# Query norms moved behind the scores, norm weights folded into the rotary tables, and one gate unit fewer in each head of an encoder kernel

## The chip, the cores and the metric

The kernel runs on one core of one Trainium2 chip. The metric is the time of one execution on the device, in microseconds; before the change its median is 1917.95 us over 3 runs (1914.27 to 1920.34).

## What is computed

One encoder layer, applied to two requests of 1024 tokens and width 1024 that share the weights ("prompt", g = 0, and "sample", g = 1). The input is normalised and modulated, and one projection `w_in` gives everything else. Branch A is attention with 8 query and 2 key heads of 64; branch B has 4 heads with two 64-wide softmax maps each and 128-wide values. Both normalise queries and keys head by head (RMSNorm with a weight) and turn them by rotary positions. Each branch is multiplied by a SiLU gate and projected, the two are merged with sigmoid gates, and a last projection with a gated residual gives the output. What the change touches:

```python
qa = rms_norm(qa.reshape(B, S, HQ_A, HEAD_DIM), qn_a)   # per head: x * rsqrt(mean(x*x) + EPS) * weight
ka = rms_norm(ka.reshape(B, S, HKV_A, HEAD_DIM), kn_a)
qa = concat(apply_rope(qa[..., :32], cos_r, sin_r), apply_rope(qa[..., 32:], cos_c, sin_c))   # ka too
oa = gqa_attention(qa, ka, va) * silu(za)               # softmax(q k / 8) v
qb = rms_norm(qb.reshape(B, S, H_B, 2, HEAD_DIM), qn_b)
kb = rms_norm(kb.reshape(B, S, H_B, 2, HEAD_DIM), kn_b)
qb = concat(apply_rope(qb[..., :16], cos_p, sin_p), qb[..., 16:])                             # kb too
ob = diff_attention(qb, kb, vb, lam)                    # (softmax(q1 k1 / 8) - lam * softmax(q2 k2 / 8)) v
```

## The kernel before

The work of a request runs in this order. **Head** (`head`): `kva_gen` projects A's keys and values, `qa_gen(st, 0)` the first four query heads of A. **Attention** (`attention`): 16 units of branch A in two halves, then 16 units of branch B, four for each head; while one half or head is attended, the projections of the next (`qa_gen(st, 1)`, `vb_gen`, `qkb_gen`) are woven in. **Then** the gating (`gated_gen`), the merge (`merge_gen`) and the output projection, `out_gen` for g = 0 and `out_seven` for g = 1. The gate projections, `z_gen`, are 48 units a request of 24 matmuls each; nothing waits for them until the gating, so they are the stock from which TensorE is kept busy wherever another chain is late. `Z_HEAD` (L41) says how many of them the head takes, `Z_SHARE` how many each phase of the attention, and what is left goes into the last phase (`fill`).

A projection (`pipelined`, L601) goes by 8 token tiles. `proj_tt` issues 24 matmuls of 128x256 for a tile (L540); `front` does the norm and the rotation on ScalarE, VectorE and GpSimd; `back`, two tiles later (`LAG` = 2), transposes the tile on TensorE and splits it into two parts (`pairs_T`, L594 to L597). In `front`, `rms` (L551) copies the tile out of PSUM (L555), squares it (L556), sums the squares by head (L559), adds EPS (L560), takes the power -0.5 on GpSimd (L561) and multiplies every head by its inverse rms (L563). Then come the norm's weight (L643 for A's keys, L662 for A's queries, L681 for B's queries and keys) and `rope`: L574 times the cosines, L582 twice times the sines, L583 the sum. L563 and what follows run on VectorE while nothing is attended (`alone`, so in the heads) and on GpSimd during attention.

A softmax unit (`softmax_unit`, L741) is one query tile of one map: four matmuls of 128x512 (L747, L748) fill one of the two `s` banks of PSUM, VectorE takes the negated row maximum (L749), ScalarE the exponential with that maximum as its bias and the row sum as a second output (L750), VectorE transposes the result (L791, after a combination at L790 in branch B), and DMAs (L800) bring it into the order that the value matmuls (L806, L823) read. There are 256 of these units.

The kernel is written as generators that `weave` interleaves by shares. A scheduler then sets the order of the instructions on each engine, and attention's steps are given a high priority there. Every engine works through its own list in order, and the DMAs are issued in order by SyncE's queue (SP). The other work of GpSimd is the split of each weight piece into two parts (L195, L237). L775 is a reciprocal of a row sum, L325 the projections of the modulation, L359, L416 and L417 its use on the activations.

Of the kernel before, what the change touches and what calls it, by code (L numbers as in the profile page):

```python
# [12 lines left out]
F32 = mybir.dt.float32  # L13
# [27 lines left out]
Z_HEAD = (4, 4)  # L41
# [48 lines left out]
def kernel(ctx: ExitStack, tc: tile.TileContext, t: dict):  # L90
# [330 lines left out]
    cosB = const.tile([P, NTT, 16], F32, name="cosB")  # L421
    sinB = const.tile([P, NTT, 16], F32, name="sinB")
# [13 lines left out]

    def load_tables_B():
# [113 lines left out]
    def rms(ps, nh, e):  # L551
# [6 lines left out]
        rs = tiny.tile([P, 4], F32, tag="rs", name=nm("rs"))[:, :nh]  # L558
# [4 lines left out]
        e.tensor_tensor(  # L563
            out=raw3, in0=raw3, in1=rs.unsqueeze(2).to_broadcast([P, nh, HD]), op=ALU.mult
        )
        return raw3, sq.rearrange("p (h d) -> p h d", d=HD)

    def rope(x3, s3, cos, sin, half, e):

        nh = x3.shape[1]  # L570
        w = x3.shape[2]
        ng = w // (2 * half)
        c3 = mtile("rc", [P, 4, HD], bufs=1)[:, :nh, :w]
        e.tensor_tensor(out=c3, in0=x3, in1=cos.unsqueeze(1).to_broadcast([P, nh, w]), op=ALU.mult)  # L574
        if ng == 1:
            x4, s4, sn = x3, s3, sin.unsqueeze(1).to_broadcast([P, nh, w])
        else:
            x4, s4 = (t.rearrange("p h (g d) -> p h g d", g=ng) for t in (x3, s3))
            sn = sin.rearrange("p (g d) -> p g d", g=ng).unsqueeze(1).to_broadcast([P, nh, ng, 2 * half])
        for a in range(2):  # L580
            o, i = (slice(b * half, (b + 1) * half) for b in (a, 1 - a))
            e.tensor_tensor(out=s4[..., o], in0=x4[..., i], in1=sn[..., o], op=ALU.mult)  # L582
        e.tensor_tensor(out=x3, in0=c3, in1=s3, op=ALU.add)  # L583
# [48 lines left out]
    def kva_gen(ht, out):  # L632
        w = kva_w.pop()[0] if kva_w else load_w(w_cols(w_in, (C_KA, 256)))
        k = v2(utile())
        va = utile().bitcast(F32)[:, :1024].rearrange("p (n k d) -> p n k d", n=NTT, k=2)
        out["ka"], out["va"] = k, va

# [15 lines left out]
    def qa_gen(st, half):  # L653
        w = load_w(w_cols(w_in, (C_QA + half * 256, 256)))
        qs = [v2(utile()), v2(utile())]
        ht = st["ht"]
        st["qa"][half] = qs

        def front(tt, ps):
            e = by_turns(tt)  # L660
            x3, s3 = rms(ps, 4, e)
            e.tensor_tensor(out=x3, in0=x3, in1=gqa.unsqueeze(1).to_broadcast([P, 4, HD]), op=ALU.mult)  # L662
            rope(x3, s3, st["cosA"][:, tt], st["sinA"][:, tt], 16, e)
            return x3
# [8 lines left out]
    def qkb_gen(ht, out, h):  # L673
        w = load_w(w_cols(w_in, (C_QB + h * P, P), (C_KB + h * P, P)))
        qk = out[h] = (v2(utile()), v2(utile()))

        def front(tt, ps):
            e = by_turns(tt)
            x3, s3 = rms(ps, 4, e)
            x4 = x3.rearrange("p (a m) d -> p a m d", a=2)  # L680
            e.tensor_tensor(out=x4, in0=x4, in1=gB.unsqueeze(2).to_broadcast([P, 2, 2, HD]), op=ALU.mult)  # L681
            rope(x3[:, :, :16], s3[:, :, :16], cosB[:, tt], sinB[:, tt], 8, e)
# [58 lines left out]
    def softmax_unit(q, sw, k, pt, su):  # L741
# [3 lines left out]
        for n in range(2):  # L745
# [3 lines left out]
        nc.vector.tensor_reduce(out=m, in_=s, axis=AX.X, op=ALU.max, negate=True)  # L749
        nc.scalar.activation(  # L750
            pt.rearrange("p (j c a) -> p j c a", j=4, c=8), s.rearrange("p (c a j) -> p j c a", c=8, j=4),
            AF.Exp, bias=m, accum_out=su,
        )

    def scores(u, i):
# [11 lines left out]
        softmax_unit(u["q"][m][:, qt * P : (qt + 1) * P], u["sw"][:, m, t * P : (t + 1) * P], u["k"][m], pt, su)  # L767
# [402 lines left out]
    def units_of(st):  # L1170

        def a_unit(half, b, pr):
# [5 lines left out]
                "pr": pr, "od": st["od"][j // 2], "su": st["suA"][:, j : j + 2],  # L1178
            }

        def b_unit(h, pr):
# [3 lines left out]
                "v": st["vb"][h], "pr": pr, "h": h,  # L1185
                "od": st["od"][4 + h], "ss": st["ssB"], "su": st["suB"][:, h],
# [38 lines left out]
    for g in range(2):  # L1225
# [21 lines left out]
        phase(1, vb_gen(ht, st["vb"], 0), qkb_gen(ht, st["qkb"], 0))  # L1247
        oT, mT = ([], []), ([], [])
        for h in range(4):
            fs = []  # L1250
            if h < 3:
                fs.append(qkb_gen(ht, st["qkb"], h + 1))
# [84 lines left out]
```

## Time and profile before

| what | value |
|---|---|
| time of 3 runs, us | 1914.27, 1917.95, 1920.34 (median 1917.95) |
| time of the profiled execution, us | 1911.4 |
| its span in the trace, us | 1909.6 |
| TensorE matmuls busy | 1847.3 us, 97% of the span |
| TensorE weight loads busy | 1553.5 us, 81% |
| VectorE (DVE) busy | 1209.3 us, 63% |
| ScalarE (ACT) busy | 771.6 us, 40% |
| GpSimd (POOL) busy | 666.6 us, 35% |
| granted TensorE clock, mean share of full speed | 0.986 |
| where things lie, us from the span's start | head of g = 0 from about 48 to 140, A's attention to about 457, B's to 765; head of g = 1 from 982 to about 1063, A's to 1360, B's to 1719 |

The profile is of one execution. A group's row gives, behind the count, the busy time in us, the mean of one instruction in ns, and the idle time of the engine just before such instructions with what ended it. In the table of waits a row says which engine and line waited for which, with the total in us, the number of waits and the longest. A tile's name stands without its number: `s` are the banks of the scores, `f` the other PSUM banks, `row` the tile under normalisation, `p` the exponentials, `m` the row maxima, `w` split weights, `u` large buffers.

### The profile page before, as it was taken

What the parts mean: (1) busy time and instruction counts of PE and PEld (TensorE: products, weight loads), DVE (VectorE), ACT (ScalarE), POOL (GpSimd) and SP (SyncE); (2) the same over time, 40 slices, a digit from 0 to 9 for tenths busy, and PEclk for the clock granted to TensorE, in tenths of its full rate; (3) what the DMA queues carried; (4) which work ended last, traced back from release to release, by engine and by line L of the source; (5) the groups of instructions that cost most, each with busy time, mean ns of one, the idle gap of its engine ahead of it and who ended that gap; (6) DMA issues with size and microseconds to landing.
All of it is one profiled execution on the core that took longest, in us unless ns stands there. A gap on an engine that the chain in (4) does not pass through costs nothing.

```text
span 1909.6 us, 29522 instructions
## 1 busy us (share of the span) xinstructions
PE 1847.3 (97%) x10398; PEld 1553.5 (81%) x10398; DVE 1209.3 (63%) x1791; ACT 771.6 (40%) x1576; POOL 666.6 (35%) x904
## 2 busy tenths in 40 slices
PE   6999999999999999999999999999999899999999
PEld 3788778888888978788888877888898798877887
DVE  5777753454876667457467787445366746674795
ACT  4545443443554444213233455344354535332241
POOL 2234511442654551221232343024474736212100
PEclk7999999999999999999999999999999999999999
DMA  9126675554443557864531567665434424586442
GB/s 320 57 84 163 186 199 159 161 151 141 111 123 104 161 152 229 281 183 156 200 107 51 146 188 196 183 182 161 138 92 115 129 70 109 163 254 211 147 126 90
DMA packets 273044, 295.04 MB, mean 155 GB/s; under 512 B 35200, under 2 KB 221696, under 8 KB 272896
## 3 DMA queue, kind: packets, MB, share of 16 engines
q1 hardware_dynamic: 272896, 293.15, 51.8%
q8 instruction: 83, 1.36, 0.3%
q14 instruction: 65, 0.53, 0.1%
HBM read 133.59 MB, written 42.01 MB: 92 GB/s over the span
## 4 chain that ended last, share of the span: by engine, by line
PE 74%; DMA 7%; DVE 6%; SPq 4%; issue 4%; POOL 3%; ACT 2%; DVEq 0%; ACTq 0%; POOLq 0%
PE f L713 20%; PE f L540 17%; PE f L985 5%; PE a L806 5%; PE s L747 5%; PE s L748 5%; PE a L823 4%; PE s L985 3%; PE f L1020 3%; SPq L800 2%; PE s L1020 2%; DMA st<-in_w_in_dram 2%; PE f L1092 2%; DVE m L749 2%; PE s L1092 1%
## 5 line engine op out<-in xcount | busy, mean ns | idle before, releaser
L713 PE MATMUL f<-u,w 128*128 128x512 f32 x2256 | 582.2, 398 | 2.7 <-POOL w L195 1.2
L713 PEld LDWEIGHTS f<-u,w 128*128 128x128 f32 x2256 | 416.5, 189 | 88.9 <-POOL w L195 2.4
L540 PE MATMUL f<-w,u 128*128 128x256 f32 x3456 | 477.8, 287 | 1.3 <-ACT w L193 0.3
L540 PEld LDWEIGHTS f<-w,u 128*128 128x128 f32 x3456 | 452.4, 192 | 22.1 <-issue 3.5
L749 DVE TENSOR_REDUCE m<-s 128x1 f32<-128x1024 f32 x256 | 310.3, 1219 | 200.0 <-PE s L748 198.0
L750 ACT ACTIVATE p<-s,m 128x1024 f32<-128x1024 f32 x256 | 285.1, 1114 | 279.0 <-DVE m L749 238.8
L195 POOL TENSOR_TENSOR w<-st,w 128x512 fp32r<-128x512 f32 x160 | 215.8, 1366 | 441.1 <-ACT w L193 424.8
L791 DVE STREAM_TRANSPOSE p<-p 128x1024 f32<-128x1024 f32 x192 | 237.6, 1241 | 58.0 <-ACT p L750 50.0
L561 POOL TENSOR_TENSOR rs<-ss,nhalf 128x4 f32<-128x4 f32 (+1 forms) x112 | 110.0, 983 | 308.7 <-DVE ss L560 271.8
L748 PE MATMUL s<-u,sw 128*128 128x512 f32 x512 | 203.8, 399 | 0.0
L193 ACT ACTIVATE w<-st 128x512 fp32r<-128x512 f32 x184 | 108.2, 627 | 98.1 <-DMA st<-in_w_in_dram 83.3
L985 PE MATMUL f<-u,w 128*128 128x512 f32 x552 | 134.8, 398 | 2.3 <-DVE u L1000 2.3
L823 PE MATMUL a<-q,u 128*128 128x256 f32 x512 | 127.0, 385 | 8.9 <-DMA q<-p 4.2
L985 PEld LDWEIGHTS f<-u,w 128*128 128x128 f32 x552 | 105.0, 192 | 24.6 <-DVE u L1000 2.5
L597 DVE TENSOR_TENSOR u<-f,u 64x256 fp32r<-64x256 f32 (+1 forms) x194 | 79.7, 411 | 71.3 <-ACT u L596 66.4
L806 PE MATMUL a<-q,u 128*64 128x256 f32 x1024 | 117.8, 382 | 2.0 <-DMA q<-p 2.0
L823 PEld LDWEIGHTS a<-q,u 128*128 128x128 f32 x512 | 95.3, 192 | 24.5 <-issue 7.6
L747 PE MATMUL s<-u 128*128 128x512 f32 x256 | 106.5, 418 | 4.9 <-ACT p L750 4.9
L748 PEld LDWEIGHTS s<-u,sw 128*128 128x128 f32 x512 | 97.2, 190 | 16.8
L790 DVE SCALAR_TENSOR_TENSOR p<-p,r,p 128x1024 f32<-128x1024 f32 x64 | 91.3, 1427 | 28.5 <-POOL r L776 26.8
L806 PEld LDWEIGHTS a<-q,u 128*64 128x64 f32 x1024 | 73.4, 137 | 40.3 <-issue 6.9
L747 PE MATMUL s<-u,u 128*128 128x512 f32 x256 | 102.9, 402 | 1.4 <-ACT p L750 1.4
(215 smaller groups left out, 2032.3 us busy)
## 6 DMA issues: line engine op xcount, KB each, us to landing
q<-p SPq DMA_DIRECT2D x768, 128.0 KB, 2.6
st<-in_w_in_dram SPq DMA_DIRECT2D x132, 256.0 KB, 3.2
zd<-ev SPq DMA_DIRECT2D x96, 256.0 KB, 2.7
sw<-u SPq DMA_DIRECT2D x256, 64.0 KB, 2.0
u<-in_w_ada_dram SPq DMA_DIRECT2D x8, 1024.0 KB, 11.4
od<-oo SPq DMA_DIRECT2D x64, 128.0 KB, 2.4
st<-in_w_in_dram SPq DMA_DIRECT2D x64, 128.0 KB, 2.7
row<-od SPq DMA_DIRECT2D x32, 256.0 KB, 2.9
```

What stands on the lines that cost most here:

```text
L195: e.tensor_tensor(out=wl, in0=st, in1=wh.bitcast(F32), op=ALU.subtract)
L540: ins = nc.tensor.matmul(ps, lt[c][:, sl], w[:, c, wi, :], start=(k == 0), stop=(k == 23))
L561: nc.gpsimd.tensor_tensor(out=rs, in0=ss, in1=nhalf[:, :nh], op=ALU.pow)
L713: ins = nc.tensor.matmul(ps, w[:, c, wi, e * P : (e + 1) * P], rt[c], start=(k == 0), stop=(k == 23),)
L747: nc.tensor.matmul(s[:, sl], q, k[:, sl], start=True, stop=False)
L748: nc.tensor.matmul(s[:, sl], sw, k[:, sl], start=False, stop=True)
L749: nc.vector.tensor_reduce(out=m, in_=s, axis=AX.X, op=ALU.max, negate=True)
L750: nc.scalar.activation(pt.rearrange("p (j c a) -> p j c a", j=4, c=8), s.rearrange("p (c a j) -> p j c a", c=8, j=4), AF.Exp, bias=m, accu ...
L791: nc.vector.transpose(pt, pt)
L806: lambda k=k, m=m: nc.tensor.matmul(acc[(LO, HI)[m]], u["v"][:, k], pT[m][:, k], start=(k == 0), stop=(k == 7))
L823: nc.tensor.matmul(acc, u["v"][:, k], pT[:, k], start=(k == 0), stop=(k == 7))
L985: nc.tensor.matmul(ps, w[:, c, wi, d * P : (d + 1) * P], o[:, oi, :], start=(k == 0), stop=(k == 11))
```

## The change

- **Queries are no longer multiplied by their inverse rms.** `rms` gets a place to keep it (`kept`) and the first head that is still multiplied (`first`): 4 of 4 for A's queries (none is), 2 of 4 in `qkb_gen` (the two key components alone). The kept values lie in the unused end of A's value buffer (`rsA`) and in a constant tile for B (`rsB`, two heads in turn).
- **The exponential gets it as its scale**, a value per row from memory, and the row maximum, its bias, is multiplied by it first: one more VectorE instruction of 128x1 in each of the 256 softmax units, between the maximum and the exponential.
- **A's query weight** is multiplied into the request's rotary tables between the keys' and the queries' use of them (`gain_tables_A`: five GpSimd instructions a request), and the product with the queries (L662) goes.
- **B's weights** for the 16 turned dimensions are multiplied into tables built for each request (`tables_B`: four DMAs and three GpSimd instructions a request; before, two DMAs in all). The tile for them comes from the pool `tab`, which holds two buffers and also A's tables. The weights of the 48 dimensions that aren't turned, the queries' and the keys', are multiplied into one factor that is put on the keys alone: 96 numbers a row where L681 multiplied 256.
- **`Z_HEAD`** goes from 4 to 3 gate units in each head, so one unit a request moves to the last phase.

```diff
-Z_HEAD = (4, 4)
+Z_HEAD = (3, 3)
...
-    cosB = const.tile([P, NTT, 16], F32, name="cosB")
-    sinB = const.tile([P, NTT, 16], F32, name="sinB")
+    rsB = const.tile([P, 2, NTT, 4], F32, name="rsB")
...
+    def gain_tables_A(st):
+
+        for name, i in (("cosA", 0), ("sinA", 1)):
+            tab = st[name]
+            if i == 0:
+                g = gqa.unsqueeze(1).to_broadcast([P, NTT, HD])
+                nc.gpsimd.tensor_tensor(out=tab, in0=tab, in1=g, op=ALU.mult)
+                continue
+            for a in range(2):
+                for b in range(2):
+                    o, x = (slice(b * 32 + c * 16, b * 32 + c * 16 + 16) for c in (a, 1 - a))
+                    g = gqa[:, x].unsqueeze(1).to_broadcast([P, NTT, 16])
+                    nc.gpsimd.tensor_tensor(out=tab[:, :, o], in0=tab[:, :, o], in1=g, op=ALU.mult)
+
+    def tables_B(st):
+
+        tab = mtile("tab", [P, 512]).rearrange("p (x n m d) -> p x n m d", x=2, n=NTT, m=2)
+        st["cosB"], st["sinB"] = cosB, sinB = tab[:, 0], tab[:, 1]
+        for dst, src in ((cosB, "cosB"), (sinB, "sinB")):
+            for i in range(2):
+                dma(dst[:, :, i], t[src].rearrange("(n p) d -> p n d", p=P))
...
     def load_tables_B():
-        for dst, src in ((cosB, "cosB"), (sinB, "sinB")):
-            dma(dst, t[src].rearrange("(n p) d -> p n d", p=P))
...
+        nc.vector.tensor_tensor(out=gB[:, 1, 16:], in0=gB[:, 1, 16:], in1=gB[:, 0, 16:], op=ALU.mult)
...
-    def rms(ps, nh, e):
+    def rms(ps, nh, e, kept=None, first=0):
...
-        rs = tiny.tile([P, 4], F32, tag="rs", name=nm("rs"))[:, :nh]
+        rs = kept if kept is not None else tiny.tile([P, 4], F32, tag="rs", name=nm("rs"))[:, :nh]
...
-        e.tensor_tensor(
-            out=raw3, in0=raw3, in1=rs.unsqueeze(2).to_broadcast([P, nh, HD]), op=ALU.mult
-        )
+        if first < nh:
+            e.tensor_tensor(
+                out=raw3[:, first:], in0=raw3[:, first:],
+                in1=rs[:, first:].unsqueeze(2).to_broadcast([P, nh - first, HD]), op=ALU.mult,
+            )
...
     def qa_gen(st, half):
...
+        if half == 0:
+            gain_tables_A(st)
...
-            x3, s3 = rms(ps, 4, e)
-            e.tensor_tensor(out=x3, in0=x3, in1=gqa.unsqueeze(1).to_broadcast([P, 4, HD]), op=ALU.mult)
+            x3, s3 = rms(ps, 4, e, st["rsA"][:, half, tt], 4)
...
-    def qkb_gen(ht, out, h):
+    def qkb_gen(st, h):
...
+        if h == 0:
+            tables_B(st)
...
-            x3, s3 = rms(ps, 4, e)
-            x4 = x3.rearrange("p (a m) d -> p a m d", a=2)
-            e.tensor_tensor(out=x4, in0=x4, in1=gB.unsqueeze(2).to_broadcast([P, 2, 2, HD]), op=ALU.mult)
-            rope(x3[:, :, :16], s3[:, :, :16], cosB[:, tt], sinB[:, tt], 8, e)
+            x3, s3 = rms(ps, 4, e, rsB[:, h % 2, tt], 2)
+            k3 = x3[:, 2:, 16:]
+            e.tensor_tensor(out=k3, in0=k3, in1=gB[:, 1:2, 16:].to_broadcast([P, 2, HD - 16]), op=ALU.mult)
+            rope(x3[:, :, :16], s3[:, :, :16], st["cosB"][:, tt], st["sinB"][:, tt], 8, e)
...
-    def softmax_unit(q, sw, k, pt, su):
+    def softmax_unit(q, sw, k, pt, su, rs):
...
         nc.vector.tensor_reduce(out=m, in_=s, axis=AX.X, op=ALU.max, negate=True)
+        nc.vector.tensor_tensor(out=m, in0=m, in1=rs, op=ALU.mult)
         nc.scalar.activation(
             pt.rearrange("p (j c a) -> p j c a", j=4, c=8), s.rearrange("p (c a j) -> p j c a", c=8, j=4),
-            AF.Exp, bias=m, accum_out=su,
+            AF.Exp, bias=m, scale=rs, accum_out=su,
         )
```

The order of the instructions shows the change at three places (line numbers are each kernel's own). The first is VectorE in the head of g = 0, one of the last query tiles of A. Before, from the sum of squares of tile `row_1224` to the end of its rotation:

```order
L559 TENSOR_REDUCE ss_1227<-row_1224 128x4
L560 TENSOR_SCALAR ss_1227<-ss_1227 128x4
L563 TENSOR_TENSOR row_1224<-row_1224,rs_1228 128x256
L597 TENSOR_TENSOR u_899<-f_1239,u_899 64x2x128
L662 TENSOR_TENSOR row_1224<-row_1224,gqa 128x256
L574 TENSOR_TENSOR rc_1234<-row_1224,tab_356 128x256
L582 TENSOR_TENSOR row_1224<-row_1224,tab_358 128x8x16 x2
L723 SCALAR_TENSOR_TENSOR ev_1308<-ev_1308,f_1208 128x512
L583 TENSOR_TENSOR row_1224<-rc_1234,row_1224 128x256
```

Now, from the start of the rotation of tile `row_1189` to its end:

```order
L613 TENSOR_TENSOR rc_1196<-row_1189,tab_355 128x256
L633 TENSOR_TENSOR u_898<-f_1201,u_898 64x2x128
L588 TENSOR_REDUCE ss_1192<-row_1189 128x4
L589 TENSOR_SCALAR ss_1192<-ss_1192 128x4
L618 TENSOR_TENSOR row_1189<-row_1189,tab_357 128x8x16 x2
L633 TENSOR_TENSOR u_899<-f_1201,u_899 64x2x128
L619 TENSOR_TENSOR row_1189<-rc_1196,row_1189 128x256
```

L563 and L662 are gone, and the rotation no longer stands behind the sum of squares and the power: its first product is ahead of them.

The second is GpSimd in the attention of g = 0, one tile of B's queries and keys. Before:

```order
L561 TENSOR_TENSOR rs_3469<-ss_3468,nhalf 128x4
L563 TENSOR_TENSOR row_3465<-row_3465,rs_3469 128x256
L681 TENSOR_TENSOR row_3465<-row_3465,gB 128x256
L574 TENSOR_TENSOR rc_3475<-row_3465,cosB 128x4x16
L582 TENSOR_TENSOR row_3465<-row_3465,sinB 128x4x8 x2
L583 TENSOR_TENSOR row_3465<-rc_3475,row_3465 128x4x16
```

Now:

```order
L590 TENSOR_TENSOR rsB<-ss_3536,nhalf 128x4
L593 TENSOR_TENSOR row_3533<-row_3533,rsB 128x128
L723 TENSOR_TENSOR row_3533<-row_3533,gB 128x2x48
L615 TENSOR_TENSOR rc_3542<-row_3533,tab_3277 128x4x16
L618 TENSOR_TENSOR row_3533<-row_3533,tab_3277 128x4x8 x2
L619 TENSOR_TENSOR row_3533<-rc_3542,row_3533 128x4x16
```

The tile has as many instructions as before; the second works on 128 numbers a row in place of 256, the third on 96.

The third is VectorE early in the attention of g = 0. Before, row maxima of three softmax units (`m`) and the transposes of two of their exponentials (`p`):

```order
L749 TENSOR_REDUCE m_1515<-s_1516 128x1
L749 TENSOR_REDUCE m_1544<-s_1545 128x1
L791 STREAM_TRANSPOSE p_1514<-p_1514 128x1024
L791 STREAM_TRANSPOSE p_1543<-p_1543 128x1024
L723 SCALAR_TENSOR_TENSOR ev_1445<-ev_1445,f_1374 128x512
L559 TENSOR_REDUCE ss_1468<-row_1465 128x4
L749 TENSOR_REDUCE m_1588<-s_1589 128x1
```

Now, with the product of maximum and inverse rms at L792:

```order
L792 TENSOR_TENSOR m_1462<-m_1462,u_360 128x1
L791 TENSOR_REDUCE m_1492<-s_1493 128x1
L792 TENSOR_TENSOR m_1492<-m_1492,u_360 128x1
L834 STREAM_TRANSPOSE p_1461<-p_1461 128x1024
L834 STREAM_TRANSPOSE p_1491<-p_1491 128x1024
L588 TENSOR_REDUCE ss_1524<-row_1521 128x4
L791 TENSOR_REDUCE m_1534<-s_1535 128x1
L589 TENSOR_SCALAR ss_1524<-ss_1524 128x4
L791 TENSOR_REDUCE m_1550<-s_1551 128x1
L792 TENSOR_TENSOR m_1534<-m_1534,u_360 128x1
L792 TENSOR_TENSOR m_1550<-m_1550,u_360 128x1
```

The product stands right behind its maximum in 69 of the 256 units (as for `m_1492`); in the others one to five instructions stand between (as for `m_1534`), in all 69 splits (L633 now, L597 before), 48 further maxima, 40 transposes, 35 sums of squares (L588, before L559) and some 60 others.

On TensorE, at the end of the head of g = 0, the transposes of the last query tile now stand behind 38 gate matmuls of 128x512 counted from that tile's last projection matmul; before, they stood behind 24 gate matmuls and 4 score matmuls.

More of the change, by code (lines that the diff above doesn't have):

```diff
@@ L435, in load_tables @@
         nc.vector.tensor_scalar(out=gqa, in0=gqa, scalar1=SC, scalar2=None, op0=ALU.mult)
+    def gain_tables_A(st):
[16 more added lines that the diff above has]
+                dma(dst[:, :, i], t[src].rearrange("(n p) d -> p n d", p=P))
+        nc.gpsimd.tensor_tensor(
+            out=cosB, in0=cosB, in1=gB[:, :, :16].unsqueeze(1).to_broadcast([P, NTT, 2, 16]), op=ALU.mult
+        )
+        for a in range(2):
+            o, i = (slice(b * 8, b * 8 + 8) for b in (a, 1 - a))
+            nc.gpsimd.tensor_tensor(
+                out=sinB[..., o], in0=sinB[..., o],
+                in1=gB[:, :, i].unsqueeze(1).to_broadcast([P, NTT, 2, 8]), op=ALU.mult,
+            )
     def load_tables_B():
-        for dst, src in ((cosB, "cosB"), (sinB, "sinB")):
-            dma(dst, t[src].rearrange("(n p) d -> p n d", p=P))
         for i, src in enumerate(("qn_b", "kn_b")):
@@ L573, in rope @@
         c3 = mtile("rc", [P, 4, HD], bufs=1)[:, :nh, :w]
-        e.tensor_tensor(out=c3, in0=x3, in1=cos.unsqueeze(1).to_broadcast([P, nh, w]), op=ALU.mult)
-        if ng == 1:
-            x4, s4, sn = x3, s3, sin.unsqueeze(1).to_broadcast([P, nh, w])
+        if len(cos.shape) == 3:
+            x4, s4, c4 = (t.rearrange("p (a m) d -> p a m d", a=2) for t in (x3, s3, c3))
+            cs, sn = (t.unsqueeze(2).to_broadcast([P, 2, nh // 2, w]) for t in (cos, sin))
         else:
             x4, s4 = (t.rearrange("p h (g d) -> p h g d", g=ng) for t in (x3, s3))
+            c4, cs = None, None
             sn = sin.rearrange("p (g d) -> p g d", g=ng).unsqueeze(1).to_broadcast([P, nh, ng, 2 * half])
+        if c4 is None:
+            e.tensor_tensor(out=c3, in0=x3, in1=cos.unsqueeze(1).to_broadcast([P, nh, w]), op=ALU.mult)
+        else:
+            e.tensor_tensor(out=c4, in0=x4, in1=cs, op=ALU.mult)
         for a in range(2):
@@ L1178, in a_unit @@
                 "pr": pr, "od": st["od"][j // 2], "su": st["suA"][:, j : j + 2],
+                "rs": [st["rsA"][:, half, :, 2 * b + i : 2 * b + i + 1] for i in range(2)],
             }
@@ L1185, in b_unit @@
                 "v": st["vb"][h], "pr": pr, "h": h,
+                "rs": [rsB[:, h % 2, :, m : m + 1] for m in range(2)],
                 "od": st["od"][4 + h], "ss": st["ssB"], "su": st["suB"][:, h],
@@ L1246 @@
         phase(0, qa_gen(st, 1))
-        phase(1, vb_gen(ht, st["vb"], 0), qkb_gen(ht, st["qkb"], 0))
+        phase(1, vb_gen(ht, st["vb"], 0), qkb_gen(st, 0))
         oT, mT = ([], []), ([], [])
@@ L1251 @@
             if h < 3:
-                fs.append(qkb_gen(ht, st["qkb"], h + 1))
+                fs.append(qkb_gen(st, h + 1))
             if h == 1:
```

10 lines of the change are left out of this document (7 added, 3 removed).

## Prediction

> **What bounds the kernel now.** I read the page first, then the table by stretches of time, then the waits of TensorE, and last the timeline around the longest of them. The page gives the span and the load of TensorE:
>
> ```profile
> span 1909.6 us, 29522 instructions
> PE 1847.3 (97%) x10398; PEld 1553.5 (81%) x10398; DVE 1209.3 (63%) x1791; ACT 771.6 (40%) x1576; POOL 666.6 (35%) x904
> ```
>
> TensorE is idle for 62.3 us in all, 1909.6 - 1847.3. The change removes no matmul, so it can win no more than that, and what TensorE loses beside it by running slowly. The stretches show where the idle time lies (columns: start and end, length, then busy us of PE, PEld, DVE, ACT and POOL, the granted clock, DMA):
>
> ```profile
> 0.00:48.00 48.00, 29.40 (x159) 17.53 (x160) 27.11 (x46) 21.24 (x40) 9.99 (x13) 0.75 0.90 319
> 96.00:144.00 48.00, 43.51 (x272) 38.66 (x271) 38.38 (x90) 19.73 (x46) 16.52 (x14) 0.96 0.29 81
> 384.00:432.00 48.00, 48.00 (x277) 39.10 (x277) 24.83 (x30) 20.84 (x44) 23.25 (x36) 1.00 0.55 155
> 720.00:768.00 48.00, 46.13 (x207) 37.98 (x205) 36.62 (x48) 20.45 (x38) 9.54 (x11) 1.00 0.75 233
> 768.00:816.00 48.00, 45.44 (x215) 37.48 (x214) 17.57 (x26) 12.74 (x23) 12.84 (x11) 1.00 0.83 285
> 1008.00:1056.00 48.00, 46.29 (x317) 42.71 (x316) 35.55 (x99) 17.94 (x52) 14.71 (x14) 1.00 0.19 57
> 1488.00:1536.00 48.00, 43.21 (x263) 37.98 (x262) 36.74 (x51) 24.18 (x52) 28.42 (x48) 0.96 0.44 120
> 1680.00:1728.00 48.00, 44.57 (x194) 36.61 (x193) 30.45 (x37) 18.71 (x34) 10.74 (x11) 0.96 0.83 260
> 1728.00:1776.00 48.00, 45.72 (x205) 37.45 (x205) 21.21 (x33) 7.18 (x13) 11.52 (x10) 0.93 0.60 192
> ```
>
> 18.6 us of it lie in the first 48 us, which the change doesn't touch. Where A is attended TensorE has no gap at all (384 to 432): an instruction taken off another engine there wins nothing. The rest is in the end of the first head, in B's attention of g = 1 and around the ends of the attentions. The waits of TensorE that bear on the change (total us, number, longest):
>
> ```profile
> PE f L594 <- DVE row L583: 7.0, 5, 3.3
> PE s L747 <- ACT p L750: 6.3, 5, 2.8
> PE f L594 <- POOL row L583: 5.0, 3, 2.6
> PEld s L747 <- ACT p L750: 10.1, 10, 3.3
> ```
>
> The first row is the rotation on VectorE, in the heads; the third the same on GpSimd, in attention; the second and fourth are scores that wait until an exponential has given its bank back.
>
> **The change part by part.** *The head of g = 0.* Two waits there belong to the last query tiles, and behind the longer one TensorE runs slowly; the timeline and the chain of waits show it, the latter also the usual pace:
>
> ```profile
> 123.86 0.44 PE L594 MATMUL f<-ident,row 128*128 128x128 f32 x2 [0.88 <-DVE row L583]
> 133.59 0.69 PE L594 MATMUL f<-ident,row 128*128 128x128 f32 x2 [3.35 <-DVE row L583]
> ```
>
> ```profile
> 134.28 5.33 PE f L713 x18
> 424.61 5.21 PE f L713 x23
> ```
>
> A matmul of 512 takes 5.33 / 18 = 296 ns after that wait and 5.21 / 23 = 227 ns otherwise, so the wait has cost 18 x 0.069 = 1.2 us more. Together 0.9 + 3.35 + 1.2 = 5.4 us. What shortens the chain to these tiles are the rows of what goes, and the power that it no longer waits for:
>
> ```profile
> L561 POOL TENSOR_TENSOR rs<-ss,nhalf 128x4 f32<-128x4 f32 x96 | 98.8, 1030 | 264.0 <-DVE ss L560 227.2 <-DVE r L775 18.7 <-ACT p L750 12.8
> L563 DVE TENSOR_TENSOR row<-row,rs 128x256 f32<-128x256 f32 x16 | 6.8, 424 | 7.4 <-POOL rs L561 7.3
> L662 DVE TENSOR_TENSOR row<-row,gqa 128x256 f32<-128x256 f32 x16 | 6.8, 422 | 0.4
> ```
>
> 1.03 + 0.42 + 0.42 = 1.9 us; and the order puts 38 matmuls ahead of the last transposes in place of 28, 10 x 0.227 = 2.3 us more cover. 4.2 us are more than 3.35, so the wait goes: **-5.4**, between -7 and -2. The lower gain is for the case that the cover, which is the gate units, runs short: VectorE saves 8 x 0.85 = 6.8 us in the head, and TensorE is left with one unit less, 24 x 0.227 = 5.4 us, to hide the rest behind. The table products are the other danger. They stand between the keys' last rotation and the queries' first and take on GpSimd one instruction of 128x512 and four of 128x128, 1.37 + 4 x 0.46 = 3.2 us by the rows below; TensorE has the projections of the next two query tiles as cover, 2 x 24 matmuls, so nothing is put down for them. In the head of g = 1, 1008 to 1056, TensorE is idle for 1.7 us, and part of that is the keys' tiles: **-0.5**, between -1.7 and 0.
>
> *GpSimd in attention.* The rows of what shrinks, and those nearest to what replaces it:
>
> ```profile
> L195 POOL TENSOR_TENSOR w<-st,w 128x512 fp32r<-128x512 f32 x160 | 215.8, 1366 | 441.1 <-ACT w L193 424.8 <-DMA st<-in_w_in_dram 14.9 <-PE s L748 1.3
> L681 POOL TENSOR_TENSOR row<-row,gB 128x256 f32<-128x256 f32 x64 | 53.3, 834 | 3.4
> L563 POOL TENSOR_TENSOR row<-row,rs 128x256 f32<-128x256 f32 x80 | 51.0, 639 | 3.6
> L574 POOL TENSOR_TENSOR rc<-row,cosB 128x64 f32<-128x64 f32 x64 | 27.5, 430 | 3.7
> L582 POOL TENSOR_TENSOR row<-row,tab 128x128 f32<-128x128 f32 x32 | 14.0, 463 | 0.0
> L662 POOL TENSOR_TENSOR row<-row,gqa 128x256 f32<-128x256 f32 x16 | 11.8, 738 | 0.9
> ```
>
> A tile of B saves 639 - 463 ns at L563 (now 128x128, as L582) and 834 - 450 at L681 (now 128x96, between L574 and L582), 0.56 us. GpSimd is relieved by 64 x 0.56 = 36 us, and by 16 x (0.64 + 0.74) = 22 us in A's second half; the tables take 2 x 3.2 and, for B, 2 x (0.83 + 2 x 0.46) = 3.5 us, so 48 of 667 us net. On the path to the end lie only the three waits of 5.0 us, each shorter by 0.56: **-1.7**, between -5 (they go, being at their threshold) and 0. In A's second half TensorE waits for nothing, so the 22 us win nothing.
>
> *The moved gate unit.* TensorE's work is the same, 5.4 us later in each request. It wins where TensorE stands idle in the end of the attention and behind it: 1.9 + 2.6 us from 720 to 816 and 3.4 + 2.3 us from 1680 to 1776, 10.1 us. Much of that is weights and gates on their way from memory, in front of the merges, and the scheduler puts gate units where attention leaves room, not there; I take a quarter, **-2.5**, between -10 and 0.
>
> *The longer softmax chain.* Between the end of a maximum and the exponential stands now an instruction of 128x1, and the exponential reads its scale from memory. The nearest rows, the last three for a bias alone, for a plain copy, and (minimum, median, maximum) for scale and bias:
>
> ```profile
> L749 DVE TENSOR_REDUCE m<-s 128x1 f32<-128x1024 f32 x256 | 310.3, 1219 | 200.0 <-PE s L748 198.0
> L791 DVE STREAM_TRANSPOSE p<-p 128x1024 f32<-128x1024 f32 x192 | 237.6, 1241 | 58.0 <-ACT p L750 50.0 <-DMA q<-p 2.6 <-DMA st<-in_w_in_dram 1.3
> L597 DVE TENSOR_TENSOR u<-f,u 64x256 fp32r<-64x256 f32 x178 | 75.1, 422 | 67.7 <-ACT u L596 63.2
> L416 ACT ACTIVATE u<-u,modc 128x512 f32<-128x512 f32 x8 | 5.4, 721 | 0.0
> L417 ACT ACTIVATE u<-u 128x512 fp32r<-128x512 f32 x8 | 4.8, 628 | 0.0
> ```
>
> ```profile
> L359 ACT ACTIVATE u<-u,modc x4: 797/807/817, 30.2 to 40.3; 128x512 f32<-128x512 f32 x4
> ```
>
> A scale from memory adds 807 - 721 = 0.09 us. The product itself has two neighbours on VectorE, a reciprocal of 128x1 and a sum of 128x4 with a constant:
>
> ```profile
> L775 DVE RECIPROCAL r<-su x64: 122/164/166, 477.8 to 1720.3; 128x1 f32<-128x1 f32 x64
> L560 DVE TENSOR_SCALAR ss<-ss x112: 121/170/1326, 52.6 to 1613.3; 128x4 f32<-128x4 f32 x96, 128x2 f32<-128x2 f32 x16
> ```
>
> ```profile
> 1511.87 1.26 POOL L195 TENSOR_TENSOR w<-st,w 128x512 fp32r<-128x512 f32 x1
> 1512.35 0.80 DVE L560 TENSOR_SCALAR ss<-ss 128x4 f32<-128x4 f32 x1
> ```
>
> The medians agree, 0.16 to 0.17 us; but L560 reaches 1.33 us, and where it took 0.80 it ended with GpSimd's L195, at 1513.1, while the reciprocal never passes 0.17. I take 0.16 for the product and 1.33 as its upper bound. [...] To this comes what stands in between in the order: 48 maxima x 1.22 + 40 transposes x 1.24 + 69 splits x 0.42 = 137 us, 0.54 us per unit on average. So an exponential starts 0.16 + 0.54 = 0.70 us later after its maximum and ends 0.79 later. VectorE gets 256 x 0.16 = 41 us more work, at 63% load. On TensorE the cost is that the bank comes back later: 15 waits are there now, 16.4 us. If each grows by 0.79, that is 11.9 us; but the order of TensorE was made anew with the product in it, and other matmuls stand ahead of the scores: **+3**, between 0 and +12 (an added step can't gain).
>
> *Tables and DMAs.* Eight small DMAs where there were two, on SP ahead of the weights of `qkb_gen`, the first of them behind A's last rotation because of the pool's two buffers; behind it on SP wait the `q<-p` pieces of running units, each with a unit's distance to its matmuls: **+0.5**, between 0 and +3.5, GpSimd's time for B's tables.
>
> The sum is -5.4 - 0.5 - 1.7 - 2.5 + 3 + 0.5 = **-6.6 us**. On the profiled execution's own 1911.4 us that gives 1904.8; this execution was 6.5 us quicker than the median of the three runs, and I carry the difference over: 1917.95 - 6.6 = **1911.3 us**. A measurement of this kernel can tell about 0.3%, 5.8 us, from no change.
>
> **The rivals.** *Slower: the softmax chain is not covered in B.* If nothing stands in for them, the 128 units of B give their banks back 0.79 us later, on two banks half of that each, 128 x 0.4 = 51 us; with gates and projections ahead of two thirds of the scores 17 us remain. With the 10.1 us of gains and the 0.5 for the tables that is +7.4, 1925.4 us. For it speaks that VectorE is busy for 36.7 of 48 us where B is attended in g = 1, so that a short product finds a queue; against it that only 15 of 256 scores wait for an exponential now. It decides from the point where TensorE's waits for exponentials pass 16.4 + 10.1 - 0.5 = 26 us.
>
> *No change: the gains are eaten.* The head's wait moves to an earlier tile, whose cover was the gate unit taken away, and the 5.4 us of that unit come back behind the attention: -5 from head and GpSimd against +5 from chain and tables, 1917.9 us. For it speaks that 48 us less on GpSimd and 14 us less on VectorE in the heads lie nearly all beside a TensorE without gaps.
>
> *More: the moved units fill the ends of both attentions* (-10 in place of -2.5) and the chain costs nothing: -6.6 - 7.5 - 3 = -17.1, 1900.8 us. For it speaks that these gaps are as long as the two units, 10.1 against 10.8 us.
>
> **How the numbers follow.** The forecast gets 0.48, slower 0.22, no change 0.20, more 0.10. The forecast's own range is 1906 to 1917. Faster by over 0.3% means under 1912.2: most of the forecast (0.41) and all of "more" make 0.51. Slower, over 1923.7, is 0.20 of its rival and 0.02 of "no change"; within 0.3% is the rest, 0.27. The range of 8 in 10 goes from a little under "more" to just over the slower rival, 1898 to 1926.
>
> **What would show it.** Right: no wait of TensorE over 1 us for the rotation between 96 and 144 us; a query tile's rotation on VectorE without the two products; 128x128 and 128x96 products on GpSimd near 0.46 and 0.45 us; exponentials of about 1.2 us, up from 1.11; TensorE's waits for them at 16 to 22 us. Wrong: those waits past 26 us, or products of 128x1 that take 0.3 us and more on average, or a new wait in the head as long as the old one.

## Result and the profile after

| | median, us | range, us | runs |
|---|---|---|---|
| before | 1917.85 | 1914.27 to 1920.34 | 4 |
| changed | 1898.93 | 1892.74 to 1902.66 | 4 |

The ratio is 0.9899, with a 95% interval of 0.9872 to 0.9927: the change wins 18.9 us, 1.0% (14 to 25 us by the interval). The forecast was 6.6 us, with a range down to 1898. The sign and the range held, but the median lies only 0.9 us inside the range, so that it held is luck; the sum was a third of the gain.

The profiled execution took 1900.7 us. Its page, the span and the line of the engines:

```profile
span 1898.9 us, 29914 instructions
PE 1843.7 (97%) x10398; PEld 1553.1 (82%) x10398; DVE 1233.2 (65%) x2016; ACT 788.4 (42%) x1576; POOL 611.0 (32%) x888
```

TensorE's idle time is 1898.9 - 1843.7 = 55.2 us, 7.1 less than before, and the same 10398 matmuls take 3.6 us less. So the profiles differ by 10.7 us. The other 8.2 of the 18.9 us lie between executions: the profiled one of before was 6.5 us under its median, that of after 1.8 over.

The same stretches of time as before, where they tell something:

```profile
96.00:144.00 48.00, 48.00 (x321) 44.05 (x320) 35.32 (x81) 22.16 (x51) 22.68 (x24) 1.00 0.36 99
720.00:768.00 48.00, 44.88 (x202) 36.80 (x200) 34.99 (x51) 17.04 (x30) 6.99 (x7) 1.00 0.78 231
768.00:816.00 48.00, 43.01 (x188) 35.36 (x189) 18.06 (x30) 14.55 (x27) 13.40 (x14) 0.93 0.73 238
1008.00:1056.00 48.00, 46.11 (x325) 42.95 (x324) 31.57 (x96) 17.27 (x54) 16.60 (x18) 1.00 0.15 45
1488.00:1536.00 48.00, 46.30 (x290) 41.60 (x289) 32.52 (x52) 22.71 (x46) 22.94 (x36) 1.00 0.42 118
1680.00:1728.00 48.00, 44.64 (x195) 36.73 (x195) 25.20 (x34) 16.40 (x29) 11.57 (x12) 0.96 0.73 226
1728.00:1776.00 48.00, 48.00 (x230) 39.87 (x229) 24.76 (x39) 8.87 (x16) 13.51 (x11) 1.00 0.60 188
```

At the end of the first head (96 to 144) TensorE has no gap any more, where 4.5 us were. Behind the attention of g = 1 (1728 to 1776) 2.3 us are gone, and in B's attention (1488 to 1536) 3.1. In the head of g = 1 nothing is won, and from 720 to 816, at the end of g = 0's attention and behind it, 3.7 us are lost.

The waits of TensorE that were shown of before (total, number, longest):

```profile
PE f L630 <- POOL row L619: 5.1, 5, 2.2
PE s L789 <- ACT p L793: 2.6, 3, 1.3
PE f L630 <- DVE row L619: 2.5, 2, 1.4
PEld s L789 <- ACT p L793: 5.1, 7, 1.7
```

Waits for the rotation on VectorE fall from 7.0 to 2.5 us, those for the rotation on GpSimd stay at 5.0 and 5.1, and those for exponentials, which the longer chain was to lengthen, fall from 6.3 to 2.6 (PE), and from 10.1 to 5.1 (PEld).

The new and the shortened instructions (the first four with minimum, median and maximum in ns; the two of GpSimd as a group's row):

```profile
L792 DVE TENSOR_TENSOR m<-m,u x128: 116/159/1194, 128.9 to 1352.7; 128x1 f32<-128x1 f32 x128
L792 DVE TENSOR_TENSOR m<-m,rsB x128: 111/159/1232, 459.0 to 1705.7; 128x1 f32<-128x1 f32 x128
L793 ACT ACTIVATE p<-s,m,u x128: 1187/1206/1212, 129.1 to 1353.0; 128x1024 f32<-128x1024 f32 x128
L793 ACT ACTIVATE p<-s,m,rsB x128: 1192/1204/1212, 459.2 to 1705.9; 128x1024 f32<-128x1024 f32 x128
```

```profile
L723 POOL TENSOR_TENSOR row<-row,gB 128x96 f32<-128x96 f32 x64 | 30.4, 474 | 3.4
L593 POOL TENSOR_TENSOR row<-row,rsB 128x128 f32<-128x128 f32 x64 | 27.4, 430 | 2.5
```

These prices came as forecast: 0.16 us for the product with rare cases up to 1.2, 1.20 for the exponential, 0.47 and 0.43 for the products on GpSimd. Of the 256 products, 42 took over 0.2 us. One of them, with GpSimd's instruction beside it (two of them in this row, the first ends at 331.88):

```profile
330.59 2.55 POOL L195 TENSOR_TENSOR w<-st,w 128x512 fp32r<-128x512 f32 x2 [0.91 <-ACT w L193]
330.70 1.19 DVE L792 TENSOR_TENSOR m<-m,u 128x1 f32<-128x1 f32 x1
```

The product ends at 331.89, with the first of the two, and each of the 42 ends 0.01 to 0.02 us behind some instruction of GpSimd (19 times L195). In this the product is like L560, which reached 1.33 us before, and not like the reciprocal of 128x1, which took 0.17 us at most in both profiles (64 of them in each).

### The profile page after: what moved, and what is told of

It reads as the page before. It is cut to its first block, busy times and chain, and to the rows that moved or that the text cites. A ratio compares the mean times of both kernels' runs of the same rounds, so it can differ in the third digit from the quotient of the medians.

```text
span 1898.9 us, 29914 instructions
## 1 busy us (share of the span) xinstructions
PE 1843.7 (97%) x10398; PEld 1553.1 (82%) x10398; DVE 1233.2 (65%) x2016; ACT 788.4 (42%) x1576; POOL 611.0 (32%) x888
## 5 line engine op out<-in xcount | busy, mean ns | idle before, releaser
L755 PE MATMUL f<-u,w 128*128 128x512 f32 x2232 | 564.9, 395 | 2.0 <-DVE w L195 1.2
L755 PEld LDWEIGHTS f<-u,w 128*128 128x128 f32 x2232 | 409.7, 188 | 84.2 <-DVE w L195 1.6
L569 PE MATMUL f<-w,u 128*128 128x256 f32 x3456 | 471.4, 285 | 2.8 <-POOL w L195 0.8
L569 PEld LDWEIGHTS f<-w,u 128*128 128x128 f32 x3456 | 447.8, 191 | 25.0 <-issue 3.3
L195 POOL TENSOR_TENSOR w<-st,w 128x512 fp32r<-128x512 f32 x160 | 212.7, 1347 | 411.3 <-ACT w L193 406.8
L793 ACT ACTIVATE p<-s,m,u 128x1024 f32<-128x1024 f32 x128 | 154.0, 1204 | 148.2 <-issue 46.9
L793 ACT ACTIVATE p<-s,m,rsB 128x1024 f32<-128x1024 f32 x128 | 153.8, 1203 | 114.1 <-DVE m L792 86.9
L1028 PE MATMUL f<-u,w 128*128 128x512 f32 x552 | 132.5, 395 | 3.6 <-DVE row L961 3.6
L1028 PEld LDWEIGHTS f<-u,w 128*128 128x128 f32 x552 | 103.7, 189 | 25.3 <-DVE row L961 3.9
L590 POOL TENSOR_TENSOR rsB<-ss,nhalf 128x4 f32<-128x4 f32 x64 | 66.9, 1046 | 154.1 <-DVE ss L589 135.7
L633 DVE TENSOR_TENSOR u<-f,u 64x256 fp32r<-64x256 f32 (+1 forms) x198 | 81.4, 411 | 52.1 <-ACT u L632 46.8
## 6 DMA issues: line engine op xcount, KB each, us to landing
u<-in_w_ada_dram SPq DMA_DIRECT2D x8, 1024.0 KB, 11.4
```

Of the source, the lines that this page charges most:

```text
L195: e.tensor_tensor(out=wl, in0=st, in1=wh.bitcast(F32), op=ALU.subtract)
L569: ins = nc.tensor.matmul(ps, lt[c][:, sl], w[:, c, wi, :], start=(k == 0), stop=(k == 23))
L755: ins = nc.tensor.matmul(ps, w[:, c, wi, e * P : (e + 1) * P], rt[c], start=(k == 0), stop=(k == 23),)
L793: nc.scalar.activation(pt.rearrange("p (j c a) -> p j c a", j=4, c=8), s.rearrange("p (c a j) -> p j c a", c=8, j=4), AF.Exp, bias=m, scal ...
L1028: nc.tensor.matmul(ps, w[:, c, wi, d * P : (d + 1) * P], o[:, oi, :], start=(k == 0), stop=(k == 11))
```

## Experiments

The theory after the result was that the work taken off GpSimd and VectorE is worth more than the three waits I had priced. The rivals: that the gate units bring the surplus (the 12 us beyond the forecast), or that the new order as a whole does and no single part. Every ratio below is against runs of the kernel before on the same chip (its medians there were 1912.7 to 1914.7 us), with its 95% interval; a difference in us is the ratio's part of that median. The changed kernel's own ratio, -19 us, comes from the runs above, on a chip that may be another.

**Parts, each in the order that the scheduler makes for it**

*Three gate units in the kernel before:*

```diff
-Z_HEAD = (4, 4)
+Z_HEAD = (3, 3)
```

> The kernel before with one gate unit fewer in each head (3, 3) and nothing else. Terms of the prediction: the head of g = 0 loses 24 x 0.227 = 5.4 us of cover in front of late rotations that are as long as before, the ends of the attentions win 2.5, so about +3 us (0 to +6) against the kernel before. If the moved units fill the ends of both attentions (the rival 'more'), -10 + 5.4 = -5 us. If the gain of 19 us is a matter of the new order as a whole and of no single part, any value between -10 and +10, and the four runs of this call do not add up to it.

Measured: 1.0064 (1.0046 to 1.0082), +12 us. Alone, this part of the change costs more than any case foresaw.

*Four gate units in the changed kernel:* the same line the other way.

> The changed kernel with the gate units back at four in each head. By the prediction's terms the units are worth 2.5 us at the ends and the head keeps its gain: 16 us faster than before where the changed kernel is 19. If the moved units are what brought the surplus over the forecast (10 us in place of 2.5), about 9 faster. If the order as a whole decides, it lies anywhere between 5 and 25 faster.

Measured: 0.9935 (0.9912 to 0.9959), -12 us, 7 less of a gain than with three. The same edit is worth +12 in one kernel and about -7 in the other; the 7 is at the edge of its noise, since the two intervals overlap a little.

*The softmax chain alone, in the kernel before:*

```diff
+        nc.vector.tensor_tensor(out=m, in0=m, in1=ones1, op=ALU.mult)
...
-            AF.Exp, bias=m, accum_out=su,
+            AF.Exp, bias=m, scale=ones1, accum_out=su,
```

> The kernel before with only the longer softmax chain: every maximum is multiplied by a constant 1 on VectorE and the exponential reads a scale of 1 from memory (same results). It prices the chain without any gain. Prediction's term: +3 us, between 0 and +12. Rival 'slower': +10 to +17, TensorE's waits for exponentials over 26 us. If the chain is free because TensorE has other matmuls ahead of the next scores, within 2 us of zero; and if the scheduler's new order matters more than the chain, it may even come out faster by some us.

Measured: 1.0006 (0.9991 to 1.0021), +1 us: free, as it stands in its own order.

*The changed kernel without the chain:*

```diff
-            x3, s3 = rms(ps, 4, e, st["rsA"][:, half, tt], 4)
+            x3, s3 = rms(ps, 4, e)
...
-            x3, s3 = rms(ps, 4, e, rsB[:, h % 2, tt], 2)
+            x3, s3 = rms(ps, 4, e)
...
-        nc.vector.tensor_tensor(out=m, in0=m, in1=rs, op=ALU.mult)
...
-            AF.Exp, bias=m, scale=rs, accum_out=su,
+            AF.Exp, bias=m, accum_out=su,
```

> The changed kernel without the longer softmax chain: queries are multiplied by their inverse rms again (one product of 128x256 on each tile of queries, 0.42 us on VectorE in the head and 0.64 on GpSimd in attention), no product behind the maximum and no scale in the exponential; tables with the weights folded in and three gate units stay. Terms of the prediction: head -4, GpSimd -0.5, gates -2.5, tables +0.5, so -6.5 against before; the chain's +3 is won back, and 1.9 of its gains are lost. If the surplus of 12 us came with the deferred inverse rms (GpSimd's waits, an order with the product in it), this run is at -6.5 or worse; if it came with the tables or the gate units, it is at -18 or better.

Measured: 0.9991 (0.9972 to 1.0009), -2 us. By this the surplus would hang on the deferred inverse rms. But the same gate units stood for +12 in one kernel and for -7 in another, so the parts are not terms of a sum, which speaks for the order.

**The order alone.** All shares with which the generators of the attention are woven, 2% up or down, and nothing else (the first row of two):

```diff
-    (1.0, 0.9, 1.1, 0.95, 1.0, 1.52),
+    (1.02, 0.918, 1.122, 0.969, 1.02, 1.55),
```

> The kernel before with every share of the attentions (ATT_W) 2% up: the same instructions, woven in a slightly different order, no part of the change. If the surplus of 12 us over the forecast is the work that the change takes off GpSimd and VectorE, an order that is only shifted stays within 4 us of the kernel before. If the order as a whole decides (rival), it is anywhere between 10 us faster and 15 slower.

> The same with every share 2% down. Less work: within 4 us of the kernel before. Order: anywhere between 10 us faster and 15 slower, and not the mirror image of the run with 2% up.

> The changed kernel with every share of the attentions 2% up. Less work: still about 19 us faster than before (15 to 23). Order: the gain falls to between 5 and 15 us, since the changed kernel's own order was one of many and the surplus came with it.

> The changed kernel with every share 2% down. Less work: about 19 us faster than before (15 to 23). Order: between 5 and 15 us faster.

| shares | before's work | changed work | changed / before |
|---|---|---|---|
| 2% up | 1.0091 (1.0077 to 1.0105) | 0.9982 (0.9972 to 0.9992) | 0.989 |
| as they are | 1 | 0.9899 (0.9872 to 0.9927) | 0.990 |
| 2% down | 0.9940 (0.9925 to 0.9956) | 0.9885 (0.9869 to 0.9901) | 0.994 |

The same instructions in another order are 11 us faster or 17 slower. This spread is wider than the effect that was forecast and than the one measured: the changed work at its worst shares (0.9982) is slower than the old work at its best (0.9940). The change is still no accident of one order: at each of the three shares it wins, 0.6 to 1.1%, about 17 us on average. (The changed kernel with shares 2% down is the fastest that was run; its interval overlaps that of the changed kernel as it is.)

**TensorE held to one order.** To price a part without the scheduler's answer to it, four kernels got edges without a semaphore between neighbouring matmuls, in the order of another kernel:

```diff
+        pe = [i for i in nc.all_instructions() if type(i).__name__.startswith("InstMatm")]
...
+        for a, b in zip(order, order[1:]):
+            tc.add_manual_dep(pe[b], pe[a].name, dep)
```

The table `order` is that of the kernel named; the other engines are ordered by the scheduler around it. Chain and gate units are edited as above; the last of the four has an edit of its own:

```diff
-    rsB = const.tile([P, 2, NTT, 4], F32, name="rsB")
+    rsB = const.tile([P, 2, NTT, 8], F32, name="rsB")
...
+        rs8 = kept
...
-        nc.gpsimd.tensor_tensor(out=rs, in0=ss, in1=nhalf[:, :nh], op=ALU.pow)
+        if alone[0] or nh < 4:
+            nc.gpsimd.tensor_tensor(out=rs, in0=ss, in1=nhalf[:, :nh], op=ALU.pow)
+        else:
+            nc.gpsimd.tensor_tensor(
+                out=rs8.rearrange("p (x h) -> p x h", x=2), in0=ss.unsqueeze(1).to_broadcast([P, 2, 4]),
+                in1=nhalf[:, :8].rearrange("p (x h) -> p x h", x=2), op=ALU.pow,
+            )
```

*The chain alone, in the order of before:*

> The kernel before with the longer softmax chain alone (a product with 1 behind each maximum, a scale of 1 from memory in each exponential), and with TensorE held to the order of the kernel before: the price of the chain with no order to help or hurt. Prediction's term: +3 us if the scheduler has put other matmuls ahead of the scores; with the old order nothing is re-arranged around the product, so up to 11.9 us, 15 waits that grow by 0.79. The rival 'slower' has +17. If the chain is covered anyway, within 2 us of zero.

Measured: 1.0201 (1.0179 to 1.0223), +38 us, where the same kernel in its own order had +1, and more than any case foresaw. The span and the line of the engines, and the first of TensorE's waits:

```profile
span 1945.5 us, 29860 instructions
PE 1858.7 (96%) x10398; PEld 1559.8 (80%) x10398; DVE 1257.8 (65%) x2048; ACT 793.3 (41%) x1576; POOL 664.9 (34%) x904
```

```profile
PE s L749 <- ACT p L753: 27.5, 24, 4.2
```

24 scores wait for an exponential, 27.5 us in all, against 5 and 6.3 us before. One of them in the kernel before, where it does not wait:

```profile
577.37 3.12 PE L540 MATMUL f<-w,u 128*128 128x256 f32 x24
580.34 0.38 PE L594 MATMUL f<-ident,row 128*128 128x128 f32 x2
580.65 0.50 PE L747 MATMUL s<-u 128*128 128x512 f32 x1
```

And the same matmul, by its place in the order, with the chain; below it VectorE's maximum of the unit that holds the bank, and its product:

```profile
586.79 3.12 PE L542 MATMUL f<-w,u 128*128 128x256 f32 x24
589.75 0.38 PE L596 MATMUL f<-ident,row 128*128 128x128 f32 x2
594.29 0.80 PE L749 MATMUL s<-u 128*128 128x512 f32 x1 [4.16 <-ACT p L753]
```

```profile
586.46 1.23 DVE L751 TENSOR_REDUCE m<-s 128x1 f32<-128x1024 f32 x1
590.75 0.16 DVE L752 TENSOR_TENSOR m<-m,ones 128x1 f32<-128x1 f32 x1
```

The maximum is there at 587.7, the product of 0.16 us comes 3 us later, behind a sum of squares, a transpose, another maximum and a split in VectorE's order.

*The changed work (four gate units), in the order of before:*

> The changed kernel with four gate units a head, and with TensorE held to the order of the kernel before, matmul for matmul (edges without semaphores between neighbours; the other engines are ordered by the scheduler around it). It takes the new order away and leaves the new work: queries not multiplied, tables, product and scale behind the maximum. If the less work on GpSimd and VectorE brings the gain of 19 us, it is 10 us or more faster than before. If the new order of TensorE brings it, within 5 us of before, by the terms of the prediction: head -2 to -5, GpSimd -1.7, chain +3, tables +0.5.

Measured: 1.0134 (1.0118 to 1.0149), +26 us. Neither answer was right: the new work in the old order is a loss. Its waits for exponentials and for the rotation:

```profile
PE s L789 <- ACT p L793: 34.4, 25, 4.2
PE f L630 <- DVE row L619: 2.5, 2, 1.4
PE f L630 <- POOL row L619: 0.9, 1, 0.9
```

The scores wait as with the chain alone, and the waits for the rotation are at 3.4 us in place of 12.0 before. Against the chain alone in the same order and on the same chip the run is 0.0067, 13 us, better: that is what the removed products are worth there, less what the tables cost.

*The old work (three gate units), in the order of the changed kernel:*

> The other half: the kernel before with three gate units a head, and with TensorE held to the order of the changed kernel. All the old work, in the new order; with its own order it was 12 us slower than before. If the less work brings the gain, it is no faster than before, 0 to +12. If the order brings it, it is 10 to 19 us faster than before.

Measured: 1.0175 (1.0159 to 1.0190), +34 us. Neither answer was right here either: the new order with the old work is a loss as well, and here the waits are those for the rotation:

```profile
PE f L594 <- POOL row L583: 21.2, 7, 7.9
PE f L594 <- DVE row L583: 10.2, 8, 3.6
```

*GpSimd's work given back, in the order of the changed kernel:*

> The changed kernel with TensorE held to its own order, and with GpSimd given back what the change takes from it: in attention the power -0.5 of a query tile runs over 8 numbers a row in place of 4, which takes 1.64 us in place of 1.03, 80 times 0.61 = 49 us, and stands in the rotation's chain as the removed products did. If GpSimd's relief brings the surplus, 8 us or more of the gain of 19 go; by the prediction's term it costs 1.7 us, at most 5.

Measured: 1.0040 (1.0026 to 1.0053), +8 us against before, so 27 us worse than the changed kernel's -19 (18.2 between the two profiles' spans, 1917.1 and 1898.9). Its engines and its first wait:

```profile
PE 1850.5 (97%) x10398; PEld 1557.1 (81%) x10398; DVE 1240.0 (65%) x2016; ACT 788.1 (41%) x1576; POOL 663.3 (35%) x888
```

```profile
PE f L637 <- POOL row L626: 17.2, 8, 4.4
```

GpSimd has 663.3 us of work, as before the change, and the rotation's waits are at 17.2 us where the changed kernel has 5.1. My term had -1.7, at most -5, for this relief.

So neither the work nor the order brings the gain by itself: each is a loss without the other, by 26 and 34 us. The scheduler fits TensorE's order to the lengths of the chains. The shorter rotation let it put transposes earlier in the heads, and the longer softmax chain made it put more ahead of the scores that had been waiting closest. The traces show both sides. In the heads, from the end of the copy out of PSUM to the tile's transposes, there are 8.4 us on average before and 7.1 after; of the kernels in their own order, the six that still multiply the queries have 8.0 to 8.6 and the four that don't 7.1 to 7.3. (In attention the same distance is 16.9 us before and 15.7 after, but 16.0 with the chain alone, so there it is not shown that the rotation moved it.) From the end of a maximum to the start of its exponential there are 0.29 us on average before, 1.44 after and 1.41 with the chain in the old order. The scores that come less than 0.5 us after the exponential has given the bank back are 14 of 254 before, 10 after, 14 with the chain in its own order, and 32 with it in the old one.

Where the time went, by stage. Each number is a stage's length less its matmuls at the usual pace (such as 227 ns for one of 512, 120 for one of 256), in us, from one profile each; B includes the stretch up to the next head:

| kernel | head g0 | A g0 | B g0 | head g1 | A g1 | B g1 | behind B g1 |
|---|---|---|---|---|---|---|---|
| before | 13.5 | 12.9 | 19.9 | 4.0 | 9.4 | 27.1 | 10.2 |
| before, 2% up | 11.5 | 19.6 | 22.6 | 3.2 | 20.2 | 29.7 | 8.2 |
| before, 2% down | 11.3 | 12.9 | 15.4 | 3.5 | 5.7 | 31.3 | 8.5 |
| before, three units | 12.8 | 13.3 | 25.7 | 5.5 | 16.0 | 35.1 | 4.6 |
| before, chain | 12.8 | 10.7 | 31.8 | 6.6 | 6.5 | 23.4 | 8.0 |
| changed | 10.0 | 12.8 | 28.9 | 3.5 | 6.8 | 19.8 | 4.5 |
| changed, 2% up | 11.2 | 9.8 | 25.9 | 6.2 | 7.5 | 29.2 | 4.4 |
| changed, 2% down | 11.5 | 9.0 | 18.8 | 8.3 | 6.2 | 22.8 | 4.4 |
| changed, four units | 11.3 | 6.2 | 22.5 | 4.0 | 9.5 | 28.8 | 6.2 |
| changed, no chain | 12.0 | 15.5 | 20.6 | 3.8 | 12.4 | 25.1 | 4.8 |

Only the last column sorts by a part of the change: 4.4 to 4.8 with three gate units in the head, 6.2 to 10.2 with four. With the order alone a stage of attention moves by 4 to 15 us in the kernel before (2% up and down), by 1 to 10 in the changed one.

## Why the prediction was right in sign and short in size

- **The bound** held: TensorE is the limit at 97%, and the gain is its idle time and the pace behind its waits. That TensorE has no gap where A is attended was read from one stretch (384 to 432); over A's attentions it is idle for 2.1 us before in g = 0 (144 to 288) and 2.8 in g = 1 (1104 to 1248).
- **Head of g = 0, -5.4:** the wait went, as the stretch from 96 to 144 shows, and with it 4.5 us of idle. In the table the stage wins 3.5. But the old order was one of the worse ones there: with shares 2% down the kernel before loses 11.3, the changed one 11.5. The term holds for this pair of orders, not for the change.
- **Head of g = 1, -0.5:** nothing, 1.7 us idle before and 1.9 after.
- **GpSimd, -1.7. This step failed.** It said that "On the path to the end lie only the three waits of 5.0 us", and that is what the profile of before shows; after, these waits are still 5.1 us. So the relief was not taken where the old trace has a wait. What the held orders show in its place: all removed products less the tables are worth 13 us in the order of before, where the sum had 7.1 for them (-5.4 - 0.5 - 1.7 + 0.5), and some 50 us of GpSimd's time (663.3 - 611.0 = 52.3 in the two profiles) are worth 27 us in the order of the changed kernel. That the scheduler turned the relief into a tighter order is the reading that fits both; in attention the traces do not show it tile by tile.
- **The gate unit, -2.5:** 5.7 us behind B's attention of g = 1 in the profile, about 7 by the run with four units. The 5.7 is from the table, slow matmuls included. The idle time that the term was to fill did not shrink: the four stretches had 10.1 us before and have 11.5 after, 2.4 less at g = 1 and 3.7 more at g = 0. In an order that does not suit it, the same edit cost 12.
- **The longer chain, +3:** +1 in an order made for it. The working was wrong twice. The delay is 1.15 us before the exponential and 0.09 in it, 1.24 in place of 0.79. Between maximum and product stand 0.80 us of other work and not 0.54, which counted splits, maxima and transposes and left out the sums of squares and the others (the trace has 35 and 93 of them, beside 48 products of other units, where the list of what stands between counts some 60). And waits do not grow by it one by one: in the forecast's own count, PE and PEld together, they fell from 16.4 to 7.7 us, where 16 to 22 were forecast. That count takes the same waits twice: all five of the PE row stand in the PEld row too, one at 1486.73 us as 0.88 and as 1.12. The rival "slower" describes what the chain does in the old order: waits far over its 26 us (27.5 on PE alone) and more than 7 us lost (38).
- **Tables, +0.5:** no wait of TensorE in the changed profile names a table.
- **The rival "more"** came nearest, 1900.8 us, with a chain that costs nothing and gate units that fill the gaps behind the attentions. Its account is right in part: the chain cost 1 us in its own order, but those gaps as a whole were not filled, and the relief of GpSimd, which it left at -1.7, is among what pays.

What stays open: how much of the 17 us between the changed kernel and the one without the chain is the deferred inverse rms and how much the luck of one order each; the pairs at shifted shares were run for the whole change only. In the held kernels TensorE alone was held, so a part of their loss may come from the orders of the other engines, as in the 3 us between maximum and product above. And no kernel was run with its own order held and nothing else changed, so it is not shown that the edges by themselves cost nothing.

## What to carry to other kernels

Where a scheduler orders the instructions anew, the waits of the old trace do not bound what shorter work can win, nor does a longer chain cost its length: here the next order spent both. Price a part with the bottleneck engine held to one order, and before a change of 1% is believed or explained, shift something that is no part of it by 2% and see how far the time moves by the order alone. Look at the change at several such orders; here it won at each of three.

## What the runs showed of the hardware

In these runs a long wait of TensorE cost more than its length. With the chain in the old order, a wait of 2.20 us and what follows it (four rows between the first and the second are left out), then two stretches of time behind it (length, then busy us of the five engines, granted clock, DMA):

```profile
615.36 0.50 PE L749 MATMUL s<-u 128*128 128x512 f32 x1 [2.20 <-ACT p L753]
617.67 0.63 PE L750 MATMUL s<-u,sw 128*128 128x512 f32 x1
618.10 0.63 PE L749 MATMUL s<-u 128*128 128x512 f32 x1
618.53 0.63 PE L750 MATMUL s<-u,sw 128*128 128x512 f32 x1
```

```profile
616.30:619.70 3.40, 2.98 (x8) 2.16 (x7) 1.95 (x4) 2.03 (x4) 0.34 (x1) 0.50 0.00 0
619.80:623.20 3.40, 3.40 (x16) 2.79 (x15) 3.19 (x5) 1.30 (x2) 0.00 (x0) 1.00 0.31 77
```

For 3.4 us the granted clock is 0.50 and matmuls of 512 start 0.43 us apart, not 0.23 as in the kernel before (5.21 us for 23 of them, from 424.61 on). Behind the first 60 us of the profiles before and after, all eleven waits of 2.17 us and more stand beside a stretch at 0.50, and none of the others, up to 1.9 us, brought one of its own. In the sum of a run: the chain in the old order has 24.5 us more idle time than before (1945.5 - 1858.7 against 62.3), and the same matmuls take 11.4 us longer, so there each us of waiting came with about half a us of slow matmuls (behind the first 60 us the clock was at 0.50 for 47.6 us, against 23.8 before). My working had this for one wait only.
